# Hymba layer on one core: w_out blocks of the FFN's first output step through the ring, and four opening sums on VectorE

## The chip, the cores and the metric

The kernel runs on 1 core of one Trainium2 chip. The metric is the device time of one launch in microseconds (us); the time before is 2031.24 us, the median of 3 runs (2028.72 to 2032.04). The core has five engines with instruction queues of their own: TensorE (PE), VectorE (DVE), ScalarE (ACT), GpSimd (POOL) and SyncE (SP); in this kernel SP issues nearly all loads.

## The reference

One layer on 1024 tokens of width 1024, with 16 meta tokens put ahead of them and dropped at the end:

```python
h = h + 0.5 * swiglu(rms_norm(h, ffn1_norm), ffn1_w_in, ffn1_w_out)
u = rms_norm(h, mix_norm) @ w_in
o = concat([hgrn2(...), stick_breaking(...)])
h = h + o @ w_out
h = h + 0.5 * swiglu(rms_norm(h, ffn2_norm), ffn2_w_in, ffn2_w_out)

def swiglu(h, w_in, w_out):
    g, u = split(h @ w_in, 2)
    return (silu(g) * u) @ w_out
```

D_MODEL is 1024, D_FF is 2816 (22 tiles of 128, so 11 pairs). All in float32.

## The kernel before

**Products.** Every large product is exact to about float32: each operand is split into an upper half (a cast to fp32r on ACT) and a lower half (source minus upper half, on DVE), and PE runs three matmuls for each product, upper by upper, lower by upper, upper by lower. A block of 512 x 128 weights by 512 tokens is 12 matmuls of 128x512.

**Both FFNs** use a scheme with 7 products in place of 8 for 2 x 2 blocks (tokens in two halves, features in two halves). The left operands are block sums of the weights (A11, A12, S1 to S4, A22), the right ones are block sums of the activations (B11, B21, T1 to T4, B22). Each FFN has an input part, `fast_in` (columns of w_in, gate and up), and an output part, `fast_out` (w_out, steps over q = 0 to 10, a pair of 128 rows each).

**`fast_out`** runs its seven steps in the order A12, A11, S1, S2, S4, S3, A22. In each step and for each q, `left` gives the left block, `right` loads the activation from DRAM, `halved` makes upper and lower halves of both, and 12 matmuls follow (line 717, tile o). The program's order is static, engine by engine; each engine works through its own queue. Three kinds of place hold left blocks: `sk` and `ak` (11 places each, one for every q) and the ring, tag "raw", with `ring_bufs` places (7 in the first FFN, 6 in the second). A block in the ring is loaded by `raw` (line 629), one in sk by line 676. The place of sk in memory is used by another pool until shortly before: tiles `both`, sums of the second FFN's w_in, which the first FFN's middle makes ahead and stores to DRAM (`w2in`). In step A12 the first three q are one batch of 36 matmuls that goes over q within each product kind (`opening`). For the first FFN the flag `apart` is set, which keeps the halves of w apart in priority from those of the activations.

**`meta`** (inside the first FFN's part, line 1876 for its matmuls) carries the 16 meta tokens along as a narrow extra product. It uses each left block as long as that lies in memory: in A12 it holds the blocks back (`held`) and multiplies all 11 after q = 10, four matmuls each.

**The opening** (`open_tokens`) loads the tokens in rows, scales them by their norm (line 761, on DVE), turns them on PE (line 770, tile xps), and makes the right operands of the first FFN while PE already works on the first columns with B11 and B21. `items` lists what DVE and ACT do ahead of each product i of that stretch: 8 to 11 are `combine(0..3)` (lines 863 and 864), 12 to 15 are `second(0..3)`, which makes `t2[j]` = b22 - b11 (line 881) and the halves of T2 and T3. `prepare(0)` loads the four blocks of the first gate column and makes its four sums s1 to s4 (line 382). It is called in item 11 and runs on POOL; in other columns of the first FFN these sums are made on DVE.

**Names for the traces.** L479, L528, L535, L538 and L539 are the DVE additions behind the products qa, qb, qc of `fast_in`; L363 is the lower half of a left block there and L361 the upper; L643 and L644 are the upper and lower halves in `fast_out` (tiles w and t in the first FFN, parts in the second); L928 makes T4's differences after the opening; L311 is the lower half of a right operand.

Of the kernel before, what the change touches and what calls it, by code (L numbers as in the profile page):

```python
# [40 lines left out]
class Block:  # L41
# [309 lines left out]
    def fast_in(self, ops, n, w_in, actD, openers, ev0, open_ev, feed=None, meta=None, spare=None,  # L351
                between=lambda: None, after_opened=lambda: None, late=lambda: None, taken=lambda at, step=True: None):

        nc = self.nc
# [22 lines left out]
        def made(x, op, y, turns):  # L377
            if turns == 2:
                t = self.early_raw.tile([P, 4, P], F32, tag="raw", name="s", bufs=4)
            else:  # L380
                t = wp.tile([P, 4, P], F32, tag="s", name="s", bufs=3)
            taken(op(t, x, y), False)
            return t
# [14 lines left out]
        prepared = {}  # L398
        quarters = (0, 0), (1, 0), (1, 1), (0, 1)

        on = nc.vector if meta else nc.gpsimd

        def first_sums(blocks, turns, on):
            a11, a21, a22, _ = blocks
            s1 = made(a21, on.tensor_add, a22, turns)
            return s1, made(s1, on.tensor_sub, a11, turns)

        def prepare(col):
            blocks = [block(i, h, col) for i, h in quarters]
            a11, a21, _, a12 = blocks  # L410
            s1, s2 = first_sums(blocks, 2, nc.gpsimd)
            s3 = made(a11, nc.gpsimd.tensor_sub, a21, 2)
            prepared[col] = blocks, (s1, s2, s3, made(a12, nc.gpsimd.tensor_sub, s2, 2))

        def weights(col, opened, turns):
            if opened and feed:
# [194 lines left out]
    def fast_out(self, hT, cs, n, w_out, actD, ready, between=lambda a, q: None,  # L611
                 meta=lambda a, q, blocks: None):

        nc = self.nc
        op, ring, pout = self.op, self.ring, self.pout
        nq = D_FF // 256
        sk = op.tile([P, nq, 512], F32, name="sk")
        ak = op.tile([P, nq, 512], F32, name="ak")

        def block(i, j, q):  # L620
            f = 2 * q + j
            return w_out[f * P : (f + 1) * P, 512 * i : 512 * i + 512]

        def fresh():
            return ring.tile([P, 512], F32, tag="raw", name="raw", bufs=self.ring_bufs)

        def raw(i, j, q):
            t = fresh()
            nc.sync.dma_start(t, block(i, j, q))
            return t  # L630

        def right(key, n):
            t = ring.tile([P, n], F32, tag="act", name="act", bufs=self.act_bufs)
            nc.sync.dma_start(t, actD[key])
            return t

        turns = {"w": 0, "t": 0}

        def halved(src, name, m):
            i = turns[name]  # L640
            turns[name] = (i + 2) % 8
            hi, lo = (self.parts[name][:, j, :m] for j in (i, i + 1))
            nc.scalar.copy(hi, src)  # L643
            at = nc.vector.tensor_sub(lo, src, hi.bitcast(F32))  # L644
            if name == "w":
                los.append(at.ins)
            return hi, lo

        sub, los = nc.vector.tensor_sub, []

        def left(step, q):

            s, a = sk[:, q, :], ak[:, q, :]
            if step == "A11":
                nc.sync.dma_start(a, block(0, 0, q))
                return a, {(0, 0): a}
            if step == "S1":
                nc.vector.tensor_add(s, raw(1, 0, q), raw(1, 1, q))
                return s, {}
            if step == "S2":  # L660
                sub(s, s, a)
                return s, {}
            if step == "S4":
                t = raw(0, 1, q)
                sub(t, t, s)
                return t, {}
            if step == "S3":
                if self.apart:
                    nc.sync.dma_start(s, block(1, 0, q))
                    u = fresh()  # L670
                    sub(u, a, s)
                    return u, {(0, 0): a, (1, 0): s}
                sub(a, a, raw(1, 0, q))
                return a, {}
            if step == "A12":
                nc.sync.dma_start(s, block(0, 1, q))
                return s, {(0, 1): s}
            t = raw(1, 1, q)
            return t, {(1, 1): t}

        banks = {}
        delayed, opening = [], []

        def evict(bank, i, j, step, ms=range(4)):
            for m in ms:
                h = hT[:, 4 * i + m, cs[j] : cs[j] + n]
                nc.vector.scalar_tensor_tensor(
                    h, banks[bank][m], 0.5, h, ALU.mult, ALU.add
                )
            if 3 in ms:  # L690
                ready(step)

        steps = [
# [4 lines left out]
        ]  # L698
        for bank, a, b, start, (i, j) in steps:
            if start:  # L700
                banks[bank] = [
                    pout.tile([P, n], F32, tag=f"{bank}{m}", name="o") for m in range(4)
                ]
            for q in range(nq):
                with self.tc.issue_after(los[-4]) if self.apart and len(los) > 4 else ExitStack():
                    src, blocks = left(a, q)
                act = right((q, b), n)
                with self.tc.high_priority() if self.apart and a == "A12" and q < 3 else ExitStack():
                    wh, wl = halved(src, "w", 512)
                    xh, xl = halved(act, "t", n)  # L710
                order = [(m, e, q, wh, wl, xh, xl) for m in range(4) for e in range(3)]
                if a == "A12" and q < 3:
                    opening += order
                    order = sorted(opening, key=lambda o: (o[1], o[2])) if q == 2 else []
                for m, e, at, wh, wl, xh, xl in order:
                    y, z = ((wh, xh), (wl, xh), (wh, xl))[e]
                    nc.tensor.matmul(  # L717
                        banks[bank][m], y[:, m * P : (m + 1) * P], z,
                        start=start and at == 0 and e == 0,
                        stop=q == nq - 1 and e == 2, skip_group_check=True,  # L720
                    )
                meta(a, q, blocks)
                between(a, q)
                if q in (1, 3) and delayed:
                    evict(*delayed[0], range(q - 1, q + 1))
                    if q == 3:
                        delayed.pop()
            if a in ("S3", "A22"):
                evict(bank, i, j, a)
            else:  # L730
                delayed.append((bank, i, j, a))
# [43 lines left out]
    def open_tokens(self, ops, opened, prepare, rows_at, ev, operands):  # L775
# [9 lines left out]
        nc, x = self.nc, self.a["x"][0]  # L785
        stt, sub = nc.vector.scalar_tensor_tensor, nc.vector.tensor_sub
# [15 lines left out]
        def apart(name, pool):  # L802
# [4 lines left out]
        t2, b11, t3 = (apart(x, temps) for x in ("t2", "b11", "t3"))  # L807
        b22 = [ev.tile([P, 512], F32, tag=x, name="b22", bufs=1 + (x == "t"))
               for x in ("t", "t", "sg01", "sg10")]
# [51 lines left out]
        def combine(j):  # L861
            ps = kept["b12"][j]
            stt(b11[j], ps, g[j], b11[j], ALU.mult, ALU.subtract)
            stt(t3[j], ps, self.ng1[:, j : j + 1], b22[j], ALU.mult, ALU.add)

        def turn_meta():
            ps = self.pin.tile([P, KT, META], F32, tag="qd", name="mps", bufs=2)
# [8 lines left out]
        def second(j):  # L876
            if j == 0:
                rows_at.close()
                pools["masks"].close()
                operands("T1", "T3", "T2")  # L880
            sub(t2[j], b22[j], b11[j])
            self.halve(ops["T2"], t2[j], j)
            return self.halve(ops["T3"], t3[j], j)

# [23 lines left out]
            7: lambda: (keep_b22(), nc.vector.tensor_copy(self.masks, sd)),  # L908
        }
        items.update({12 + j: lambda j=j: second(j) for j in range(4)})  # L910
        items.update({8 + j: lambda j=j: combine(j) for j in range(3)})
        items[11] = lambda: (prepare(0), combine(3))
        after = {6: turn_b22, 7: turn_b12, 8: turn_meta}
        for i in range(2, len(order)):
            if i + 2 < len(order):
# [761 lines left out]
    def run(self):  # L1677
        nc, tc, a = self.nc, self.tc, self.a
# [20 lines left out]
        with ExitStack() as c0:  # L1699
            with ExitStack() as c1:  # L1700
# [8 lines left out]
                with tc.manual_schedule(engines={nc.tensor.engine}), ExitStack() as c2:  # L1709
# [98 lines left out]
                    opened, prepare = next(steps)  # L1808
# [13 lines left out]
                with tc.manual_schedule(engines={nc.tensor.engine}), ExitStack() as c2:  # L1822
# [59 lines left out]
                    last_q = D_FF // 256 - 1  # L1882
# [3 lines left out]
                    def meta(step, q, blocks):  # L1886
# [1 line left out]
                        if step not in banks_at:  # L1888
                            return
                        held.extend((i, j, q, t) for (i, j), t in blocks.items())  # L1890
                        if q < last_q and (step != "A22" or q % 3 < 2):
                            return
                        for i, j, at, t in sorted(held, key=lambda x: x[0]):
                            new = at == 0 and i in banks_at[step]
# [230 lines left out]
            with tc.manual_schedule(engines={nc.tensor.engine}), ExitStack() as cx:  # L2125
# [91 lines left out]
                made = feed()  # L2217
# [65 lines left out]
```

## Time and profile before

| | |
|---|---|
| runs | 2032.04, 2028.72, 2031.24 us |
| profiled execution | 2028.28 us, of which the span from the first to the last instruction is 2026.3 |
| granted TensorE clock, mean | 0.994 |
| w_in blocks of the first FFN's ring loads, us to landing (median) | 3.9 |
| w_out blocks: ring loads / sk loads (median) | 4.3 / 5.2 |

A line of the profile names the source line, engine, operation and tiles (out<-in) with their shapes, how often, the busy time and the mean of one, and after the bar the idle time ahead of it with what ended that. "SPq" is a DMA issue on SP's queue; "DMA x<-y" is the transfer itself. PEclk is the clock granted to TensorE, 1.00 being full speed. In a timeline a row holds the start, the duration, and the group of equal instructions that follow one another.

### The profile page before, as it was taken

The numbers are of one execution on the slowest core, as the hardware profiler recorded it, in microseconds if no ns is written. First come the engines' busy times: TensorE is split into PE (matmuls) and PEld (weight loads), VectorE is DVE, ScalarE is ACT, GpSimd is POOL, SyncE is SP. The second block draws the span as 40 slices with busy tenths as digits, with TensorE's granted clock in tenths as the row PEclk, the third lists the DMA queues.
The fourth block names the chain that finished last, engine by engine and source line by source line (L and its number), as shares of the span: only waits on it lengthen the run. The fifth ranks groups of instructions, "written<-read, shape, count | busy, mean of one in ns | idle before, by whom it ended". The sixth has DMA issues, their size and how long they took to land.

```text
span 2026.3 us, 30704 instructions
## 1 busy us (share of the span) xinstructions
PE 1960.7 (97%) x10940; PEld 1650.1 (81%) x10940; DVE 1364.6 (67%) x2136; ACT 860.6 (42%) x1731; POOL 462.6 (23%) x608
## 2 busy tenths in 40 slices
PE   7999999997999999999999999999999999989998
PEld 6788888885888888888888978877888888878887
DVE  7977777775578663247777667567566766757674
ACT  6523443333444444456666635433133332334443
POOL 4010100010000002233333331320544544520000
PEclk9999999998999999999999999999999999989999
DMA  6256787758955326344454166665533323278363
GB/s 205 86 160 170 250 272 244 236 182 306 331 189 187 126 70 188 129 160 116 123 144 138 50 255 175 165 220 178 185 98 104 111 94 104 98 264 291 112 200 135
DMA packets 315576, 347.16 MB, mean 171 GB/s; under 512 B 61520, under 2 KB 216656, under 8 KB 315424
## 3 DMA queue, kind: packets, MB, share of 16 engines
q1 hardware_dynamic: 297136, 292.18, 45.8%
q0 software_dynamic: 17248, 53.03, 7.6%
q8 instruction: 86, 1.41, 0.3%
q14 instruction: 66, 0.54, 0.1%
q10 hardware_dynamic: 1040, 0.00, 0.0%
HBM read 233.75 MB, written 111.38 MB: 170 GB/s over the span
## 4 chain that ended last, share of the span: by engine, by line
PE 90%; DVE 4%; DMA 3%; ACT 1%; issue 1%; SPq 0%; DVEq 0%; ACTq 0%
PE o L717 21%; PE qb L447 17%; PE qa L447 12%; PE qc L447 11%; PE proj L250 5%; PE proj L252 5%; PE proj L251 5%; PE flip L1409 2%; PE wo L250 1%; PE wo L251 1%; PE wo L252 1%; PE lvl L1202 1%; PE oacc L1479 1%; PE oacc L1481 1%; PE mq L981 1%; PE z L1545 1%
## 5 line engine op out<-in xcount | busy, mean ns | idle before, releaser
L447 PE MATMUL qb<-T,wh 128*128 128x512 f32 x1056 | 345.0, 391 | 2.6 <-DVE u L479 1.3
L447 PEld LDWEIGHTS qb<-T,wh 128*128 128x128 f32 x1056 | 198.2, 188 | 47.8 <-issue 2.5
L447 PE MATMUL qa<-B,wh 128*128 128x512 f32 x696 | 226.9, 391 | 0.3 <-ACT B L820 0.2
L717 PE MATMUL o<-t,w 128*128 128x512 f32 x924 | 213.0, 392 | 14.1 <-ACT w L643 14.1
L717 PE MATMUL o<-parts 128*128 128x512 f32 x924 | 212.8, 393 | 6.4 <-ACT parts L643 6.4
L250 PE MATMUL proj<-xh,wh 128*128 128x512 f32 (+2 forms) x640 | 216.7, 339 | 0.8 <-DVE st L1102 0.7
L717 PEld LDWEIGHTS o<-t,w 128*128 128x128 f32 x924 | 174.1, 189 | 51.0 <-ACT w L643 14.2
L252 PE MATMUL proj<-xl,wh 128*128 128x512 f32 (+2 forms) x640 | 209.9, 328 | 0.8 <-DVE xl L1864 0.8
L717 PEld LDWEIGHTS o<-parts 128*128 128x128 f32 x924 | 175.4, 190 | 43.4 <-ACT parts L643 6.8
L251 PE MATMUL proj<-xh,wl 128*128 128x512 f32 (+2 forms) x640 | 210.1, 328 | 0.0
L447 PE MATMUL qb<-T,wl 128*128 128x512 f32 x528 | 205.9, 390 | 1.2 <-DVE wl L363 1.2
L363 DVE TENSOR_TENSOR wl<-s,wh 128x512 fp32r<-128x512 f32 x160 | 165.8, 1036 | 50.2 <-ACT wh L361 49.2
L361 ACT CAST wh<-s 128x512 fp32r<-128x512 f32 x160 | 99.3, 622 | 194.1 <-PE qb L447 154.3
L447 PEld LDWEIGHTS qa<-B,wh 128*128 128x128 f32 x696 | 130.6, 188 | 27.9 <-DVE B L821 0.5
L361 ACT CAST wh<-raw 128x512 fp32r<-128x512 f32 x120 | 74.4, 621 | 147.3 <-PE qc L447 106.3
L447 PE MATMUL qa<-B,wl 128*128 128x512 f32 x348 | 135.6, 390 | 0.0
L252 PEld LDWEIGHTS proj<-xl,wh 128*128 128x128 f32 x640 | 120.7, 189 | 12.1 <-DVE xl L1864 1.2
L250 PEld LDWEIGHTS proj<-xh,wh 128*128 128x128 f32 x640 | 120.9, 189 | 11.3 <-DVE st L1102 1.2
L251 PEld LDWEIGHTS proj<-xh,wl 128*128 128x128 f32 x640 | 120.8, 189 | 9.0
L447 PE MATMUL qc<-B,wh 128*128 128x512 f32 x352 | 115.2, 391 | 2.2 <-DVE u L538 2.2
L447 PE MATMUL qc<-T,wh 128*128 128x512 f32 x352 | 117.2, 394 | 0.0
L447 PEld LDWEIGHTS qb<-T,wl 128*128 128x128 f32 x528 | 99.2, 188 | 21.6 <-DVE wl L363 1.6
(395 smaller groups left out, 3906.6 us busy)
## 6 DMA issues: line engine op xcount, KB each, us to landing
raw<-in_ffn_w_in_dram SPq DMA_DIRECT2D x176, 256.0 KB, 3.9
raw<-in_ffn_w_out_dram SPq DMA_DIRECT2D x99, 256.0 KB, 4.3
w2in<-both SPq DMA_DIRECT2D x28, 512.0 KB, 3.4
raw<-in_w_in_dram SPq DMA_DIRECT2D x25, 512.0 KB, 4.1
sk<-in_ffn_w_out_dram SPq DMA_DIRECT2D x33, 256.0 KB, 5.2
ks<-kD SPq DMA_DIRECT2D x32, 260.0 KB, 4.8
wout<-both SPq DMA_DIRECT2D x16, 512.0 KB, 3.6
wh<-w2in SPq DMA_DIRECT2D x27, 256.0 KB, 3.5
```

The costliest lines, as they stand in the source:

```text
L250: nc.tensor.matmul(ps, wh[:, s], xs, start=k == 0, stop=False)
L251: nc.tensor.matmul(ps, wl[:, s], xs, start=False, stop=False)
L252: nc.tensor.matmul(ps, wh[:, s], xl[:, k, c0 : c0 + n], start=False, stop=k == nk - 1)
L361: nc.scalar.copy(hi, src)
L363: nc.vector.tensor_sub(lo, src, hi.bitcast(F32))
L447: nc.tensor.matmul(ps, a[:, k, :], b[:, k, :], start=start and k == 0 and i == 0, stop=k == 3 and i == 2, skip_group_check=True,)
L717: nc.tensor.matmul(banks[bank][m], y[:, m * P : (m + 1) * P], z, start=start and at == 0 and e == 0, stop=q == nq - 1 and e == 2, skip_gro ...
L981: nc.tensor.matmul(ps[at : at + 32, at_g, :], self.xm[:, 4 * h + k, :], got[i, h][:, k, :], start=h == 0 and kk == 0, stop=h == 1 and kk = ...
L1202: nc.tensor.matmul(ps[:, :, c, :], kp[:, P * c : P * c + P], strided(QA, P * c + n, (512 - n, 2), (2 * n, nb), (1, n)), start=True, stop=True,
L1409: self.nc.tensor.transpose(ps[:m, j, :], src[:, s0 : s0 + m], self.ident)
L1479: nc.tensor.matmul(o[:, c], vj, w[0], start=j == 0, stop=False, skip_group_check=True)
L1481: nc.tensor.matmul(o[:64, c], vj[:, :64], w[1], start=False, stop=end, skip_group_check=True)
```

## The change

Three things are changed. (1) In step A12 of `fast_out`, the block of q goes to the ring by `raw(0, 1, q)` as long as q < `ring_bufs`, and to sk only from there on. (2) The meta tokens' matmuls of A12 are also issued after q = `ring_bufs` - 1, for the blocks held until then. (3) In the opening, `prepare(0)` is a generator that runs on `on`, which is DVE in the first FFN; `combine(0)`, `combine(1)` and `combine(2)` each take it one step further (loads with s1 and s2; s3; s4), and `combine(1..3)` make `t2[0..2]`, so `second` makes only `t2[3]`.

```diff
@@ prepare
-            s1, s2 = first_sums(blocks, 2, nc.gpsimd)
-            s3 = made(a11, nc.gpsimd.tensor_sub, a21, 2)
-            prepared[col] = blocks, (s1, s2, s3, made(a12, nc.gpsimd.tensor_sub, s2, 2))
+            s1, s2 = first_sums(blocks, 2, on)
+            yield
+            s3 = made(a11, on.tensor_sub, a21, 2)
+            yield
+            prepared[col] = blocks, (s1, s2, s3, made(a12, on.tensor_sub, s2, 2))
+            yield
@@ left
             if step == "A12":
-                nc.sync.dma_start(s, block(0, 1, q))
-                return s, {(0, 1): s}
+                if q >= self.ring_bufs:
+                    nc.sync.dma_start(s, block(0, 1, q))
+                    return s, {(0, 1): s}
+                t = raw(0, 1, q)
+                return t, {(0, 1): t}
@@ combine
             stt(t3[j], ps, self.ng1[:, j : j + 1], b22[j], ALU.mult, ALU.add)
+            if j:
+                sub(t2[j - 1], b22[j - 1], b11[j - 1])
+            if j < 3:
+                next(prepared)
@@ second
-            sub(t2[j], b22[j], b11[j])
+            if j == 3:
+                sub(t2[j], b22[j], b11[j])
@@ items
-        items.update({8 + j: lambda j=j: combine(j) for j in range(3)})
-        items[11] = lambda: (prepare(0), combine(3))
+        items.update({8 + j: lambda j=j: combine(j) for j in range(4)})
+        prepared = prepare(0)
@@ meta
-                        if q < last_q and (step != "A22" or q % 3 < 2):
+                        if q < last_q and (step, q) != ("A12", self.ring_bufs - 1) and (
+                            step != "A22" or q % 3 < 2
+                        ):
                             return
```

## The prediction

> **What bounds the kernel now.** I read the page first: the busy times, the chain that ended last, and the costliest groups with the idle time ahead of them.
>
> ```profile
> PE 1960.7 (97%) x10940; PEld 1650.1 (81%) x10940; DVE 1364.6 (67%) x2136; ACT 860.6 (42%) x1731; POOL 462.6 (23%) x608
> ...
> PE 90%; DVE 4%; DMA 3%; ACT 1%; issue 1%; SPq 0%; DVEq 0%; ACTq 0%
> ...
> L717 PE MATMUL o<-t,w 128*128 128x512 f32 x924 | 213.0, 392 | 14.1 <-ACT w L643 14.1
> L717 PE MATMUL o<-parts 128*128 128x512 f32 x924 | 212.8, 393 | 6.4 <-ACT parts L643 6.4
> ```
>
> TensorE (PE) is busy 97% of the 2026.3 us, so only some 65 us of idle time can be won at all. Two groups carry a lot of it: the w_out matmuls of the first FFN (tiles t, w) and of the second (parts). Each of the two amounts is one single wait, at the start of its step A12. Next I read, around the first, the waits (who waited for what: us in total, times, longest) and the chain.
>
> ```profile
> ACT w L643 <- DMA sk<-in_ffn_w_out_dram: 12.4, 1, 12.4
> ```
>
> ```profile
> 481.24 5.60 DMA w2in<-both
> ...
> 486.99 4.76 DMA sk<-in_ffn_w_out_dram
> ...
> 492.44 31.67 PE o L717 x132
> 524.11 2.54 PE m L1876 x88
> ```
>
> PE waits for a cast, the cast for the block's load into sk, and that load is issued only when a store of w2in has ended: the place of sk in memory is still being read by that store. The queue of SP and the last PE work ahead of the gap complete the picture (start, duration, what):
>
> ```profile
> 461.76 0.37 SPq L634 DMA_DIRECT2D act<-act10B  x1
> ...
> 468.68 4.01 SPq L629 DMA_DIRECT2D raw<-in_ffn_w_out_dram  x5
> ...
> 486.99 6.42 SPq L676 DMA_DIRECT2D sk<-in_ffn_w_out_dram  x11
> ```
>
> ```profile
> 477.82 0.53 PE L959 MATMUL mf<-pick,mt 128*128 128x32 f32 x4
> 492.44 31.67 PE L717 MATMUL o<-t,w 128*128 128x512 f32 x132 [14.09 <-ACT w L643]
> ```
>
> The ring already takes five blocks of w_out at 468.68, for the third step, S1, which is over 60 us away; the blocks that are needed at once come 18 us later.
>
> **The first transition, part by part.** After the change the blocks q = 0 to 6 of A12 go to the ring (seven buffers) by line 629, and SP's new order puts raw 0 into the slot of the first right-hand load, at 461.76, and the others between the next ones, all issued by about 472.5. Their landing, from the view of DMA issues over 455 to 500 us:
>
> ```profile
> raw<-in_ffn_w_out_dram SPq DMA_DIRECT2D x5, 256.0 KB, 5.3
> ```
>
> So all seven are there by 472.5 + 5.3 = 477.8, and the first three, which are enough for the opening 36 matmuls, by about 474, ahead of PE's end at 478.35. What is late next? The banks. Their last readers on VectorE (DVE) are these:
>
> ```profile
> 472.58 0.69 DVE L538 TENSOR_TENSOR u<-qc,u 128x512 f32<-128x512 f32 x1 [3.70 <-PE qc L447]
> ...
> 479.19 0.69 DVE L538 TENSOR_TENSOR u<-qc,u 128x512 f32<-128x512 f32 x1
> ```
>
> In the changed program's order DVE also takes three lower halves of w ahead of them, 3 x 0.6 = 1.8 us, which fit in its 3.70 us of idle time before 472.58 as far as the loads are early enough. The last bank is then free at 479.19 + 0.69 = 479.88 as before, at best 0.6 earlier, at worst 1.8 later. The first bank is free earlier, so PE starts between 478.7 and 480; I take a gap of 0.7 us, since only the last of four banks binds. The gap goes from 14.09 to 0.7: -13.4 (bounds -12.1 and -13.8).
>
> Next the granted clock after that gap. The columns are PE busy (matmuls), weight loads, DVE, ACT, POOL, the clock, the DMA share and GB/s:
>
> ```profile
> 492.00:494.00 2.00, 1.56 (x4) 1.28 (x5) 1.58 (x3) 1.90 (x4) 0.00 (x0) 0.50 1.05 387
> 494.00:496.00 2.00, 2.00 (x7) 1.57 (x6) 1.06 (x2) 0.34 (x1) 0.00 (x0) 0.60 1.04 393
> 496.00:498.00 2.00, 2.00 (x10) 1.64 (x10) 0.00 (x0) 0.10 (x1) 0.00 (x0) 1.00 1.05 399
> ```
>
> After 14 us of idleness PE runs at 0.50, and 132 matmuls take 31.67 us. One x512 matmul at full clock takes 0.227 us (12 in the 2.72 us of a block), so 132 would take 29.9: the cold start costs 1.7 us, and a gap of 0.7 us should not cause it. Some matmuls may also have waited for w in that time, so the bounds are 1.0 and 1.8. [...]
>
> Two more moves cost nothing by the rows, with their covers. The 28 of the 44 meta matmuls that move from behind q = 10 to behind q = 6 (the trace has two records for each, x88 in 2.54 us, so 1.6 us of it) are the same work on PE, at another place; they only need blocks that lie in the ring already. And the last four sk loads still wait for the w2in store until about 487 and land some 5 us later, 492; block 7 is wanted at 479 + 7 x 2.72 + 1.6 = 499.7. The cover is 7 us; gone, each us late is one us of PE.
>
> **The second transition.** fast_out is shared, and nothing in the condition asks for the first FFN. With the second FFN's ring of six buffers, q = 0 to 5 go to the ring there too. The rows:
>
> ```profile
> 1777.77 0.34 SPq L634 DMA_DIRECT2D act<-act0B  x1
> ...
> 1792.59 0.89 SPq L676 DMA_DIRECT2D sk<-in_ffn_w_out_dram  x1
> ```
>
> ```profile
> 1793.67 0.39 PE L447 MATMUL qc<-B,wh 128*128 128x512 f32 x1
> ```
>
> ```profile
> 1799.78 0.62 ACT L643 CAST parts<-sk 128x512 fp32r<-128x512 f32 x1 [10.78 <-DMA sk<-in_ffn_w_out_dram]
> ```
>
> ```profile
> 1794.09 0.69 DVE L538 TENSOR_TENSOR u<-qc,u 128x512 f32<-128x512 f32 x1 [1.30 <-PE qc L447]
> ```
>
> PE ends at 1794.06 and waits 6.4 us for a block whose load was issued at 1792.59. Raw 0 takes the slot at 1777.77, ahead of the first right-hand load; all six are issued by about 1788 and land before PE ends. The last bank is free at 1794.78, so the gap becomes 0.7: -5.7 (bounds -4.5 and -6.4). Its clock:
>
> ```profile
> 1800.00:1802.00 2.00, 1.55 (x4) 1.27 (x5) 1.54 (x3) 1.01 (x2) 1.22 (x3) 0.50 1.04 409
> 1802.00:1804.00 2.00, 2.00 (x6) 1.54 (x5) 1.97 (x3) 1.00 (x2) 1.04 (x1) 0.50 1.05 406
> 1804.00:1806.00 2.00, 2.00 (x6) 1.59 (x5) 1.47 (x2) 0.24 (x1) 0.86 (x2) 0.50 1.04 413
> 1806.00:1808.00 2.00, 2.00 (x9) 1.59 (x9) 0.00 (x0) 0.62 (x1) 0.00 (x0) 0.92 1.05 404
> ```
>
> In these 8 us PE runs 25 matmuls in 7.55 us of busy time, where 25 x 0.227 = 5.7 would do, and the next slice is still filling up; against full pace from 1800.45 on (118 matmuls in 29.8 us where 26.8 would do) it is 3.0 (bounds 1.9 and 3.0).
>
> **The opening.** Four sums of the first gate leave POOL. The rows of DVE, POOL and PE around them:
>
> ```profile
> 34.78 1.38 DVE L761 TENSOR_SCALAR row<-row,ss_x 128x1024 f32<-128x1024 f32 x2
> ...
> 36.70 3.43 DVE L761 TENSOR_SCALAR row<-row,ss_x 128x1024 f32<-128x1024 f32 x2
> ```
>
> ```profile
> 41.23 2.87 POOL L382 TENSOR_TENSOR s<-raw,s 128x512 f32<-128x512 f32 x1
> ```
>
> ```profile
> 38.50 0.66 PE L770 MATMUL xps<-ident,row 128*128 128x128 f32 x4 [1.00 <-DVE row L761]
> 40.18 0.66 PE L770 MATMUL xps<-ident,row 128*128 128x128 f32 x4 [1.02 <-DVE row L761]
> ```
>
> DVE scales a row of 1024 in 0.7 us until POOL starts its sums at 35.8, and in 1.7 us beside them; PE waits twice 1.0 us for these rows. Without POOL's sums, both waits should go: -2.0 (bounds 0, if something else slowed the rows, and -2.1).
>
> DVE gets four sums (0.6 us each back to back) and gets three of T2's differences earlier: 7 x 0.6 = 4.2 us more between 45 and 58, and 1.8 us fewer after 58.
>
> ```profile
> 40.00:50.00 10.00, 9.82 (x58) 8.23 (x59) 6.71 (x11) 4.15 (x7) 4.67 (x3) 1.00 0.27 79
> ...
> 60.00:70.00 10.00, 10.00 (x46) 8.29 (x45) 9.83 (x16) 7.84 (x16) 0.00 (x0) 1.00 0.22 62
> 70.00:80.00 10.00, 7.56 (x33) 5.62 (x32) 9.90 (x22) 5.35 (x11) 0.54 (x1) 1.00 0.06 26
> ```
>
> ```profile
> 58.71 0.69 DVE L881 TENSOR_TENSOR t<-b,b 128x512 f32<-128x512 f32 x1
> ```
>
> ```profile
> 74.73 0.50 PE L447 MATMUL qb<-T,wh 128*128 128x512 f32 x1 [1.28 <-DVE u L479]
> ...
> 79.12 0.50 PE L447 MATMUL qb<-T,wl 128*128 128x512 f32 x1 [1.16 <-DVE wl L363]
> ```
>
> DVE has 3.3 us idle in 40 to 50 and is full from 60 to 80, where PE waits 1.28 and 1.16 us for it. So the earlier work lies in idle time, and the full stretch gets 1.8 us shorter. But there DVE's order is changed as well: the lower half (line 363) that ended the second wait now stands behind two more subtractions of line 928 and a second u (line 479). I expect the two short waits to be replaced by one of about 2.5 us: net 0 (bounds -2.4, both gone, and +1.2, two more 0.6 us operations in front). The four block loads, too, move ahead of three on SP; those three are needed from 49 us on, and the queue has half its time free here, so 0.
>
> **The sum.** -2.0 - 13.4 - 1.7 - 5.7 - 3.0 = -25.8. The profiled execution took 2028.28 (its span of 2026.3 and 2.0 around it), 2.96 below the median of 2031.24. Its sum is 2002.5; set against the median I forecast 2005.4, say 2005. With all bounds at their best, -27.1 - 2.4 = -29.5 gives 2002 or, from the lowest run of 2028.72, 1999; at their worst, -19.5 + 1.2 = -18.3 gives 2013.
>
> **The rivals.** (1) Only the first transition closes, because the change is named for that FFN, or because DMA, at a share of 1.04 from 1800 on, still lands the second's blocks late. Against it: the SP slots from 1777.77 on lie well before that rush. Then 2031.24 - 17.1 = 2014. (2) The opening backfires: a sum waits on DVE for its block, all behind it waits too, and PE loses 2.5 us more and gains none of the 2.0: 2005.4 + 4.5 = 2010. [...] (3) The change does not do what it says: the loads are early, but PE restarts on the right-hand operand or a bank, and half of each gap (7.0 and 3.2) and the cold clock stay: 2031.24 - 10.2 - 2.0 = 2019. (4) Slower: S1 starves. The ring is now full of A12's blocks until q = 6, and S1's two blocks for each q, five of which were early before, are all loaded later. If only one pair were in flight, each of S1's 11 blocks would take 5.3 (landing) + 0.69 (sum) + 0.62 + 0.69 (halves) = 7.3 us against 2.72 on PE: +50 in the first FFN, 2005.4 + 50 = 2055. It decides when a pair takes over 2.72 + 25.8 / 11 = 5.1 us. Against it: six or seven buffers are three pairs in flight, 2.4 us a pair, and before, with 17 of the 22 blocks loaded at pace, the groups of line 717 show no wait but the two at their start.
>
> **How the numbers follow.** Chances: forecast 0.70, (1) 0.10, (2) 0.09, (3) 0.04, (4) 0.05, and 0.02 that gains and losses cancel. Faster by over 0.2% (4 us, about what a measurement tells from no change): 0.93; within: 0.02; slower: 0.05. The forecast's own range with the runs' scatter is 1999 to 2013; to take in (1) with the same scatter, 1999 to 2017.
>
> **What would show it.** Right: line 717's two groups with under 1.5 us of idle time each, clock 1.00 in the slices after both starts, no line 382 on POOL before 45 us and line 761 at 0.7 us throughout, a wait of 2 to 3 us near 75. Wrong: line 717 with a new releaser in steps S1 (DVE sk from raw, DMA raw), a wait of PE for line 363 in 45 to 58, or sk blocks 7 to 10 late.

## The result and the profile after

| | before | after |
|---|---|---|
| median of the runs beside each other, us | 2031.28 (2028.72 to 2032.04, 4 runs) | 2002.57 (2001.04 to 2003.36, 4 runs) |
| ratio, 95% interval | | 0.986 (0.9843 to 0.9877) |
| profiled execution / its span, us | 2028.28 / 2026.3 | 2002.59 / 2000.7 |
| mean granted clock | 0.994 | 0.999 |

The forecast was 2005 (1999 to 2017). Span against span the change takes 25.6 us off. The page of the changed kernel: busy times, chain, and the two groups of w_out matmuls (line 717 is line 723 now).

```profile
PE 1956.6 (98%) x10940; PEld 1646.5 (82%) x10940; DVE 1362.6 (68%) x2140; ACT 860.7 (43%) x1731; POOL 455.3 (23%) x604
...
PE 91%; DVE 4%; DMA 2%; ACT 1%; issue 1%; POOL 0%; SPq 0%; DVEq 0%; ACTq 0%
...
L723 PE MATMUL o<-t,w 128*128 128x512 f32 x924 | 212.1, 390 | 0.5 <-DVE u L541 0.5
...
L723 PE MATMUL o<-parts 128*128 128x512 f32 x924 | 209.9, 389 | 0.0
```

The idle time ahead of the first FFN's group fell from 14.1 to 0.5 us, that of the second from 6.4 to nothing. PE's busy time fell too, by 4.1 us for the same 10940 matmuls: the mean granted clock rose from 0.994 to 0.999. SP's queue and the chain of waits at the first transition (start, duration, what):

```profile
458.29 0.38 SPq L632 DMA_DIRECT2D raw<-in_ffn_w_out_dram  x1
460.93 0.32 SPq L637 DMA_DIRECT2D act<-act10B  x1
...
468.71 0.91 SPq L632 DMA_DIRECT2D raw<-in_ffn_w_out_dram  x2
...
485.23 0.88 SPq L680 DMA_DIRECT2D sk<-in_ffn_w_out_dram  x2
```

```profile
474.52 0.69 DVE u L541
...
475.34 8.86 PE o L723 x38
...
484.23 10.73 PE o L723 x46
494.96 1.67 PE m L1887 x56
496.63 11.12 PE o L723 x48
```

The seven ring loads are issued between 458.3 and 469.6, among the right-hand loads. No DMA stands in this chain any more: what PE waits for is the last reader of a bank on VectorE, 0.5 us. The sk loads are as late as they were (485 against 487), but nobody stands behind them. The meta tokens' matmuls are in two parts, 56 records at 494.96 and 32 later.

The clock behind both starts, at 475.34 and 1777.69 (columns as in the prediction's tables of stretches):

```profile
474.00:476.00 2.00, 1.52 (x10) 1.27 (x9) 2.00 (x4) 0.20 (x1) 0.54 (x1) 1.00 0.85 264
```

```profile
1778.00:1780.00 2.00, 2.00 (x11) 1.65 (x10) 1.67 (x3) 0.00 (x0) 0.22 (x2) 1.00 1.04 403
```

It stays at 1.00. DMA works at a share of about 1.0 as before, but PE no longer waits for it there.

In the opening, rows of DVE and of PE:

```profile
36.73 1.40 DVE L767 TENSOR_SCALAR row<-row,ss_x 128x1024 f32<-128x1024 f32 x2
```

```profile
36.50 2.34 PE L776 MATMUL xps<-ident,row 128*128 128x128 f32 x16
...
74.28 0.50 PE L450 MATMUL qb<-T,wl 128*128 128x512 f32 x1 [2.68 <-DVE wl L363]
```

Two rows are scaled in 1.40 us where they took 3.43, and PE's 16 matmuls that turn the four rows follow without a wait. Near 75 us one wait of 2.68 us has taken the place of 1.28 and 1.16.

### The profile page after: what moved, and what is told of

Same layout as the page of the kernel before. It is cut to its first block, busy times and chain, and to the rows that moved or that the text cites. A ratio compares the mean times of both kernels' runs of the same rounds, so it can differ in the third digit from the quotient of the medians.

```text
span 2000.7 us, 30716 instructions
## 1 busy us (share of the span) xinstructions
PE 1956.6 (98%) x10940; PEld 1646.5 (82%) x10940; DVE 1362.6 (68%) x2140; ACT 860.7 (43%) x1731; POOL 455.3 (23%) x604
## 4 chain that ended last, share of the span: by engine, by line
PE 91%; DVE 4%; DMA 2%; ACT 1%; issue 1%; POOL 0%; SPq 0%; DVEq 0%; ACTq 0%
PE o L723 21%; PE qb L450 17%; PE qc L450 12%; PE qa L450 12%; PE proj L250 5%; PE proj L252 5%; PE proj L251 5%; PE flip L1420 2%; PE wo L250 1%; PE wo L251 1%; PE wo L252 1%; PE mq L992 1%; PE lvl L1213 1%; PE oacc L1490 1%; PE oacc L1492 1%; PE z L1556 1%
## 5 line engine op out<-in xcount | busy, mean ns | idle before, releaser
L723 PE MATMUL o<-t,w 128*128 128x512 f32 x924 | 212.1, 390 | 0.5 <-DVE u L541 0.5
L723 PE MATMUL o<-parts 128*128 128x512 f32 x924 | 209.9, 389 | 0.0
L251 PE MATMUL proj<-xh,wl 128*128 128x512 f32 (+2 forms) x640 | 209.9, 328 | 0.0
L450 PE MATMUL qb<-T,wl 128*128 128x512 f32 x528 | 205.7, 390 | 2.7 <-DVE wl L363 2.7
```

The source lines that it names most:

```text
L251: nc.tensor.matmul(ps, wl[:, s], xs, start=False, stop=False)
L450: nc.tensor.matmul(ps, a[:, k, :], b[:, k, :], start=start and k == 0 and i == 0, stop=k == 3 and i == 2, skip_group_check=True,)
L723: nc.tensor.matmul(banks[bank][m], y[:, m * P : (m + 1) * P], z, start=start and at == 0 and e == 0, stop=q == nq - 1 and e == 2, skip_gro ...
```

## The experiments

The chips differ a little: the kernel before has a median of 2030.24 us (19 runs) beside the first four, 2033.18 (7 runs) beside the second four, and 2028.74 (7 runs) beside the last three. So ratios are compared, and spans where one execution's places are read. An edit is shown against the changed kernel's lines, and only in part where it says so.

| run | median us | ratio to before (95%) |
|---|---|---|
| first FFN's ring only | 2015.58 | 0.9929 (0.9915 to 0.9944) |
| second FFN's ring only | 2020.64 | 0.9955 (0.9940 to 0.9969) |
| opening only | 2028.52 | 0.9994 (0.9984 to 1.0005) |
| opening only, T2's differences late | 2028.41 | 0.9988 (0.9978 to 0.9997) |
| three blocks in the first ring | 2012.44 | 0.9905 (0.9887 to 0.9923) |
| meta matmuls not earlier | 2002.77 | 0.9859 (0.9842 to 0.9876) |
| T4's differences on GpSimd | 2002.69 | 0.9859 (0.9838 to 0.9880) |
| changed, T2's differences late | 2002.16 | 0.9851 (0.9833 to 0.9870) |
| one lower half first | 2004.43 | 0.9882 (0.9866 to 0.9899) |
| sums on GpSimd again | 2003.90 | 0.9883 (0.9868 to 0.9898) |
| changed kernel again | 2003.09 | 0.9884 (0.9868 to 0.9900) |

### One part at a time

The ring in the first FFN alone, with the opening as before (the one line of the ring is shown):

```diff
-                if q >= self.ring_bufs:
+                if not self.apart or q >= self.ring_bufs:
```

> The kernel before, with A12's early blocks in the ring (and the meta tokens' earlier matmuls) in the first FFN alone; opening and second FFN as before. Theory (the three gains are independent and each is what its own place shows): the wait of 14.1 us at the first w_out step becomes under 1 us and the cold clock behind it goes, 1.7 us; the 6.4 us at the second stay; 15.3 us less than before, about 2016. Rival (most of the gain sits in one place, since an earlier first FFN also moves the loads behind it): 20 us or more less, and the second wait shrinks without an edit.

```profile
L720 PE MATMUL o<-parts 128*128 128x512 f32 x924 | 212.5, 393 | 6.9 <-ACT parts L643 6.9
...
L720 PE MATMUL o<-t,w 128*128 128x512 f32 x924 | 212.0, 391 | 0.5 <-DVE u L538 0.5
```

The time is 0.71% less, 14.4 us of 2030.24, against 15.3 expected. The second wait stays, at 6.9 us: nothing shrinks there without its own edit, and the rival falls.

The ring in the second FFN alone, with the opening and the meta matmuls as before (again the one line):

```diff
-                if q >= self.ring_bufs:
+                if self.apart or q >= self.ring_bufs:
```

> The kernel before, with A12's early blocks in the ring in the second FFN alone. Theory: the wait of 6.4 us goes to 0 and some 2 to 3 us of half clock with it; 8 to 9.4 us less than before, about 2022.5, and the 14.1 us of the first stay. Rival (the half clock was no consequence of the wait, or the early start is given back later in that FFN): 6.4 us less or fewer, 2025 or above, with a clock of 0.5 or a new wait behind the start.

```profile
L720 PE MATMUL o<-t,w 128*128 128x512 f32 x924 | 213.4, 393 | 13.9 <-ACT w L643 13.9
...
L720 PE MATMUL o<-parts 128*128 128x512 f32 x924 | 209.9, 390 | 0.0
```

9.1 us less (0.45% of 2030.24). The wait of 6.4 us is gone, and the group's busy time fell from 212.8 to 209.9: 2.9 us more. That is the clock: in the profile before, PE works 5.86 us at 0.50 behind this wait, which is 2.9 us too long. The second FFN, which the change's name does not mention, is worth a third of the whole.

The opening alone (A12 and the meta matmuls as before), and the same with T2's differences left in `second` (that part of the edit is shown further down, under the changed kernel with T2's differences late):

```diff
-                if q >= self.ring_bufs:
+                if True:
...
-                        if q < last_q and (step, q) != ("A12", self.ring_bufs - 1) and (
-                            step != "A22" or q % 3 < 2
-                        ):
+                        if q < last_q and (step != "A22" or q % 3 < 2):
```

> The kernel before with the opening's edit alone (sums on VectorE in three steps, three of T2's differences early). Theory: the two waits of 1.0 us for scaled rows go, since GpSimd does no sums beside them; the two waits of 1.28 and 1.16 us near 75 us become one of 2.7; in all 2 us less, about 2029.3. Rival (what helps is the shorter stretch of VectorE after 58 us, from the early differences): the waits for rows stay, those near 75 us go.

> As the kernel with the opening's edit alone, but T2's differences stay where they were (behind the combinations, with the halves). Theory: the rows are scaled in 0.7 us all the same, as GpSimd's sums are gone (2.0 us gained before 41 us), but VectorE's full stretch from 58 us on is 1.8 us longer, so the wait near 75 us grows from 2.7 to about 4.5 us: about 2031, no gain. Rival (the differences' place does not matter, because VectorE makes the time up): the wait stays at 2.7 us and the time at 2029.

In both, PE's waits for rows are gone. Opening alone near 75 us, PE's row, and the chain behind the wait in this kernel (second fence) and in the changed one (third):

```profile
74.69 0.80 PE L450 MATMUL qb<-T,wl 128*128 128x512 f32 x1 [2.68 <-DVE wl L363]
```

```profile
74.69 7.04 PE qb L450 x23
```

```profile
74.28 5.53 PE qb L450 x23
```

The wait is the one of 2.7 us that was expected, and the changed kernel's profile has the same one. But here the clock falls to 0.50 behind it, from 74.6 to 78.0, and there it stays at 1.00: the same 23 matmuls take 7.04 us here and 5.53 there, so the clock cost 1.5 us in this execution. How the idle time lies in the two is in the last section.

With T2's differences late, PE's waits between 20 and 100 us, and the two groups:

```profile
PE qb L450 <- DVE u L482: 1.3, 1, 1.3
PE qb L450 <- DVE wl L363: 1.2, 1, 1.2
```

```profile
L723 PE MATMUL o<-t,w 128*128 128x512 f32 x924 | 213.6, 393 | 14.8 <-ACT w L646 14.8
L723 PE MATMUL o<-parts 128*128 128x512 f32 x924 | 212.3, 392 | 7.1 <-ACT parts L646 7.1
```

Neither theory nor rival is right: the wait near 75 us is neither 4.5 nor 2.7 but again 1.3 and 1.2, as before the change. VectorE makes up four more sums with its idle time; it is the early differences, not the sums, that turn two waits into one. The ratio 0.9988 is 2.4 us of 2030.24 (0.6 to 4.5), so the 2 us of the rows can be there in full; the 0.9994 of the opening alone is 1.2 us (-1.0 to 3.2). In this profile the two transitions wait 14.8 and 7.1 us, 0.7 more each than before, in that of the opening alone 13.7 and 6.0; one profile each does not say what moves them.

### What the ring must cover

Only three blocks in the first FFN's ring:

```diff
-                if q >= self.ring_bufs:
+                if q >= (3 if self.apart else self.ring_bufs):
```

> The changed kernel, but in the first FFN only the blocks q = 0 to 2 of A12 go to the ring and q = 3 to 10 to sk. Theory (it is the sk blocks, held up by the w2in stores until about 485 us, that set when PE can go on; the ring must cover the time until then): PE starts A12 at 475 as in the changed kernel, does 36 matmuls in 8.2 us, then waits some 5 to 8 us for block 3, and since that is longer than the clock lasts, PE runs at half clock again after it for 1.7 us; 2002.6 + 7 to 10, about 2011. Rival (three blocks are enough, the others only fill the ring): 2003.

```profile
476.99 8.41 PE L723 MATMUL o<-t,w 128*128 128x512 f32 x36 [0.48 <-DVE u L541]
492.69 13.26 PE L723 MATMUL o<-t,w 128*128 128x512 f32 x48 [7.29 <-ACT w L646]
```

```profile
488.00:490.00 2.00, 0.00 (x0) 0.00 (x0) 0.00 (x0) 0.00 (x0) 0.00 (x0) 0.99 1.12 379
490.00:492.00 2.00, 0.00 (x0) 0.00 (x0) 0.00 (x0) 0.00 (x0) 0.00 (x0) 0.50 0.92 320
```

As the theory had it: the start after the same wait of 0.5 us (in this execution 1.65 us later than in the changed kernel's), 36 matmuls, then 7.3 us for block 3 out of sk, and a cold clock (the group's busy time is 214.2 against 212.1). Together that is 9.4 us; the ratio is 0.45% above the changed kernel's, 9.1 us. PE idles from 485.4; the clock falls at 490. Three blocks gain the start and lose it 8 us later: the ring has to last until the sk blocks are there, at 492. At 2.72 us a block three more would have covered the 7.3 us, an estimate from these rows; four to six blocks were not tried.

### The ring's earlier release

The meta matmuls of A12 all behind q = 10 again (the edit of `meta` alone undone, as above):

> The changed kernel without the extra place for the meta tokens' matmuls: all 44 follow q = 10 again, so the seven ring buffers are held until then, some 11 us longer, and the third step's blocks can be loaded only later. Theory: the third step's first pair is wanted over 20 us after that, so nothing waits: 2002.6, same. Rival (this earlier release is what keeps the third step from starving, the slower case of the prediction): a wait of w_out matmuls for VectorE's sums or ring loads at the third step, 2 us or more slower.

Ring loads after A12 in this kernel (first row) and in the changed one (second row):

```profile
511.02 0.93 SPq L632 DMA_DIRECT2D raw<-in_ffn_w_out_dram  x2
```

```profile
505.39 0.96 SPq L632 DMA_DIRECT2D raw<-in_ffn_w_out_dram  x2
```

S1's loads start 5.6 us later, and the time is the same, 0.9859. The group of line 723 has 0.6 us of idle time in all. S1 does not starve, and this part of the change is worth nothing measurable.

### VectorE near 75 us

The changed kernel with T4's four differences on GpSimd:

```diff
-                    sub(b21[j], b21[j], t2[j])
+                    nc.gpsimd.tensor_sub(b21[j], b21[j], t2[j])
```

> The changed kernel with the four differences for T4 in the opening (b21 minus t2) on GpSimd, which is idle there, in place of VectorE. Theory (VectorE's amount of work between 58 and 90 us is what makes the one wait of 2.7 us): 2.4 us less on VectorE, the wait shrinks to 0.3 or less, 2 to 2.4 us faster, about 2000.3; GpSimd's operations (1.3 to 2 us each) end well before T4's halves are made. Rival (two-input work on GpSimd slows VectorE's operations beside it, as it did with the scaled rows): VectorE's operations beside it take over 0.8 us, and the wait stays or grows, 2002.6 to 2005.

```profile
54.46 1.61 POOL L939 TENSOR_TENSOR b<-b,t 128x512 f32<-128x512 f32 x1 [2.61 <-DVE t L872]
...
65.94 3.48 POOL L939 TENSOR_TENSOR b<-b,t 128x512 f32<-128x512 f32 x1 [5.54 <-DVE t L892]
```

```profile
54.84 1.78 DVE L363 TENSOR_TENSOR wl<-raw,wh 128x512 fp32r<-128x512 f32 x1
...
66.98 1.28 DVE L311 TENSOR_TENSOR T<-t,T 128x512 fp32r<-128x512 f32 x2
```

```profile
59.28 0.47 PE L450 MATMUL qa<-B,wh 128*128 128x512 f32 x1 [1.26 <-ACT wh L361]
```

Both happen. The wait of 2.7 shrinks to 0.3, so VectorE's amount of work did make it. But GpSimd takes each difference as soon as it can, from 50 us on; a lower half on VectorE beside it takes 1.78 us where it takes 0.68, and PE loses 1.26 us near 59, to an upper half on ScalarE that the changed kernel does not wait for (how the slowed operations make that one late was not followed). At 65.94 it is the other way: GpSimd's operation takes 3.48 us, where the others take 1.28 to 1.61, and VectorE's keep 0.6 each. What is left, 1.1 us, is below what the runs can tell: 0.9859 against 0.986.

The changed kernel with T2's differences late:

```diff
-            if j:
-                sub(t2[j - 1], b22[j - 1], b11[j - 1])
...
-            if j == 3:
-                sub(t2[j], b22[j], b11[j])
+            sub(t2[j], b22[j], b11[j])
```

> The changed kernel, but T2's differences stay where they were before (sums on VectorE, both rings). Theory (the early differences only turn two short waits near 75 us into one long one): waits of 1.3 and 1.2 us in place of 2.7, the time within 0.5 us of the changed kernel, 2002.4. Rival (now that nothing later swallows it, the early differences gain the 1.8 us that leave VectorE's full stretch): 2004.4.

```profile
PE qb L450 <- DVE u L482: 1.2, 1, 1.2
PE qb L450 <- DVE wl L363: 1.2, 1, 1.2
```

0.9851 against 0.986 of the changed kernel: no difference that the intervals tell. The early differences gain nothing here either.

The changed kernel with priority for the one lower half that PE waits for:

```diff
-            nc.vector.tensor_sub(lo, src, hi.bitcast(F32))
+            with self.tc.high_priority() if first_now[0] else ExitStack():
+                nc.vector.tensor_sub(lo, src, hi.bitcast(F32))
...
+                first_now[0] = bool(meta and opened and op == "T3")
                 left = ready.pop(0) if ready else next(w)
+                first_now[0] = False
```

> The changed kernel, with one lower half of a left block (line 363, the one that PE waits 2.7 us for near 74 us) given priority on VectorE, so that it comes ahead of the last halves of T1 and the differences for T4; no operation is added or moved to another engine. Theory (that wait is VectorE's order, not its amount of work: the operand was there early and stood behind four operations that nobody needed yet): the wait falls below 0.7 us and no other of over 1 us comes in its place before 100 us; 2 us faster than the changed kernel, 2000.5. Rival (VectorE is simply full until 90 us, so the 2.7 us come back at the next thing that it is late with): the same sum of PE's waits between 60 and 100 us, 2002.5.

```profile
76.86 0.54 PE L452 MATMUL qb<-T,wh 128*128 128x512 f32 x1 [2.09 <-ACT wh L361]
77.96 0.80 PE L452 MATMUL qb<-T,wl 128*128 128x512 f32 x1 [0.56 <-DVE wl L364]
```

```profile
77.17:84.00 6.83, 6.26 (x15) 4.79 (x15) 4.68 (x9) 3.99 (x8) 0.00 (x0) 0.50 0.00 0
```

The rival is right: the wait moves on by one product, to the next block's halves, with 2.09 + 0.56 = 2.65 us in place of 2.68. That block's sum (line 384 there) stands behind the postponed differences. In this execution the clock fell as well, for 6.8 us. Together with the smaller wait when T4's differences leave VectorE, this says that VectorE has more to do in this stretch than fits, and that the order only chooses what is late.

The changed kernel with the sums on GpSimd, in the same three places of the program:

```diff
-            s1, s2 = first_sums(blocks, 2, on)
+            s1, s2 = first_sums(blocks, 2, nc.gpsimd)
...
-            s3 = made(a11, on.tensor_sub, a21, 2)
+            s3 = made(a11, nc.gpsimd.tensor_sub, a21, 2)
...
-            prepared[col] = blocks, (s1, s2, s3, made(a12, on.tensor_sub, s2, 2))
+            prepared[col] = blocks, (s1, s2, s3, made(a12, nc.gpsimd.tensor_sub, s2, 2))
```

> The changed kernel with the first gate's four sums on GpSimd again, but in the changed places (behind the combinations, after the rows are scaled). Theory (what gains 2 us in the opening is that GpSimd does not work beside the scaling of the rows; which engine makes the sums is second): PE's waits for rows stay at 0; GpSimd's sums now run beside VectorE's two-input operations and slow some of them from 0.7 to 1.4 or 1.8 us, as the differences for T4 on GpSimd did, and that costs PE 0 to 2 us: 2002.5 to 2004.5. Rival (VectorE is the place that matters: with 2.4 us taken off it again, the wait of 2.7 us goes): 2000.

```profile
28.90 1.74 POOL L382 TENSOR_TENSOR s<-raw 128x512 f32<-128x512 f32 x1
30.61 2.25 POOL L382 TENSOR_TENSOR s<-raw,s 128x512 f32<-128x512 f32 x1
```

```profile
29.42 2.31 DVE L752 SCALAR_TENSOR_TENSOR junk<-row 128x1024 uint8<-128x1024 f32 x1
```

```profile
32.48 0.47 PE L450 MATMUL qa<-B,wh 128*128 128x512 f32 x1 [1.09 <-DVE sg L538]
```

The time lies within the theory's range (0.9883 beside 0.9884 for the changed kernel on the same chip), but the sums did not run where I had put them. GpSimd's queue is nearly empty, so it starts as soon as the blocks are there, at 26 us, now ahead of the scaling and beside the rows' sums of squares, one of which takes 2.31 us in place of 1.22. PE waits 1.09 us for what stands behind it, and still 2.37 near 75. The rows themselves are scaled at 0.7 us each, after GpSimd's last sum (it ends at 32.9), so what slows them in the kernel before is that GpSimd works beside them, not which engine makes the sums.

The changed kernel itself, beside the last two:

> The changed kernel itself, beside the two others on this chip. Every theory: 2002.6, one wait of 2.7 us near 74 us; whether the clock falls behind that wait may differ from the first profile (where it stayed 1.00), as it did in the kernel with the opening's edit alone (0.70).

```profile
74.02 0.50 PE L450 MATMUL qb<-T,wl 128*128 128x512 f32 x1 [2.69 <-DVE wl L363]
```

The same wait and, in this execution too, a clock of 1.00. No version tried is faster than the changed kernel beyond its interval.

## Why the prediction was right

**The sum.** Span against span, by terms: first wait 14.1 to 0.5, second 6.4 to 0, rows 2.0 to 0, the waits near 75 us 2.4 to 2.7, PE's busy time 4.1 less: -13.6 - 6.4 - 2.0 + 0.2 - 4.1 = -25.9, where the span shows -25.6 and -25.8 was forecast. That it comes so close is in part luck: 0.8 us too much for the first cold clock and 0.7 too little for the second wait cancel. The median moved by 28.7, since the profiled execution of before was faster than each of the four timed runs; beside the last three kernels the same change gives 1.16% of 2028.74, 23.5 us. The size is known to some 3 us, no better.

**First transition.** Forecast -13.4 for the wait, measured -13.6; the bank on VectorE is what is late next, as worked out. For the cold clock 1.7 was forecast, and the group's busy time fell by 0.9 only (213.0 to 212.1), just under my lower bound of 1.0. The clock itself cost what I had taken for it. In the profile before:

```profile
492.44:495.59 3.15, 3.15 (x8) 2.48 (x8) 2.62 (x4) 1.82 (x3) 0.00 (x0) 0.50 1.06 395
```

3.15 us at half the clock are 1.6 us lost, and the blocks behind them run at 2.72 us each. What I had at nothing is the rest: at a clock of 1.00 the changed kernel's first 132 matmuls take 8.86 + 10.73 + 11.12 = 30.7 us, not 29.9. About 0.3 us is a stop behind the 38th (484.23, a weight load that waits 0.4 us for VectorE's lower half of t), and about 0.3 the place where the meta tokens' matmuls now part the step once more, both estimates from the starts of the matmuls. So the move of the meta matmuls is not quite free, but it costs too little for the runs to tell. (The bound of -12.1 for the wait does not follow from its rows either: 1.8 us later than the 0.7 is a gap of 2.5, so -11.6.)

**Second transition.** Forecast -5.7 and -3.0, measured -6.4 and -2.9. The bank that I had expected to cost 0.7 us cost nothing. The 2.9 is what this wait cost in the one execution that I had sized it from: in the three other profiles that have the wait (first ring only, opening alone, opening with late differences) the group's busy time is 2.6, 1.8 and 2.4 above 209.9, for waits of 6.9, 6.0 and 7.1 us.

**Opening.** Rows: -2.0 forecast and measured, and the kernels without the ring show it too. That GpSimd's work beside VectorE was the reason is borne out by the two kernels that put some back: an operation of VectorE beside it took up to 1.9 (2.31 against 1.22 us) and 2.6 times as long (1.78 against 0.68), and the rows, scaled when GpSimd had ended, kept their 0.7 us. With T4's differences on GpSimd, VectorE's operation took 1.78 us at 54.84, where GpSimd had begun first (54.46), and GpSimd's took 3.48 us at 65.94, where VectorE had (65.78); what decides which of the two is slowed was not tried. The scaling of the rows is shown to slow down by its own rows alone (two in 1.38 us ahead of GpSimd's sums, two in 3.43 beside them). The exchange of two short waits for one of 2.5 us was right at 2.68. My reason for it was wrong in part: I had the sums and the differences together as work that shortens or fills VectorE's stretch; the run with late differences shows that the sums cost nothing and that the differences alone change the order.

**Rivals.** (1) falls with the second ring alone. (2), a wait of VectorE for a block, did not come. (3) falls with both groups. (4), a starving S1, has no sign even when its loads start 5.6 us later still; how late is too late was not tried.

**Not settled:** what the opening alone is worth in the time (0.9994, where its rows gain 2 us). The clock behind the one wait, 1.5 us where it falls, would account for the difference, and three of its ten runs have a mean clock of 0.992, which none has with late differences; but the intervals of the two kernels overlap. What moves the waits of the two transitions by up to 0.7 us between profiles is open as well.

## What to carry to other kernels

Where the matrix engine stands still at the seam of two phases, ask what holds the place that the first block is loaded to: a few blocks in buffers that are free early do for the whole seam, if they last until the held places come free, and shortage shows as the same wait a few blocks later. Count the cold clock with each such wait (half the clock cost 1.6 us behind the one of 14.1 us here, 2.9 behind the one of 6.4), and do not join two short waits into one long one for nothing: the long one, 2.68 us, cost the clock 1.5 us in the opening alone, where the two of 1.3 and 1.2 did not. An edit of the order in a stretch where VectorE is full only moved the wait here, 2.65 us in place of 2.68. Work that went to an idle GpSimd ran when its inputs had landed (from 26.3 us the sums, from 50.3 the differences), not where the program has it, and while it and VectorE ran side by side, one slowed the other (1.78 us in place of 0.68 on VectorE, 3.48 in place of 1.28 to 1.61 on GpSimd).

## What the runs showed of the hardware

**Where the granted clock changed.** The wait of 2.68 us (or 2.69) near 75 us stands in five profiles. The clock stayed at 1.00 in three (changed kernel, changed again, three blocks) and fell for 3.41 us in two (opening alone, meta matmuls not earlier): PE's two qb groups are busy 344.3 to 344.7 and 205.6 to 205.7 us in the three, 345.5 to 345.8 and 206.4 to 206.6 in the two. In the profile of the kernel before, the clock is 0.50 from 481.94 to 495.59 and from 1796.07 to 1806.31; those are four and three steps of 3.413 us, and from the first fall to the second there are 385. In opening alone it is 0.50 from 74.60 to 78.02, one step, in one lower half first from 77.17 to 84.00, two. So in these three profiles the changes lie on a grid of 3.413 us. Laid over PE's work (its busy time is the first number behind the comma, in us), here is one step each of six profiles, in this order: opening alone (with the cold step behind it), meta matmuls not earlier, changed, changed again, before, and first ring only:

```profile
71.19:74.60 3.41, 0.82 (x4) 0.36 (x2) 3.41 (x7) 1.78 (x3) 0.00 (x0) 1.00 0.00 0
74.60:78.02 3.42, 3.33 (x8) 2.69 (x9) 3.05 (x6) 1.66 (x3) 0.00 (x0) 0.50 0.00 0
```

```profile
71.88:75.29 3.41, 1.36 (x6) 1.14 (x7) 3.41 (x7) 1.58 (x4) 0.00 (x0) 1.00 0.00 0
```

```profile
72.85:76.26 3.41, 1.98 (x9) 1.64 (x10) 3.41 (x7) 1.96 (x4) 0.00 (x0) 1.00 0.00 0
```

```profile
72.32:75.73 3.41, 1.71 (x7) 1.42 (x8) 3.41 (x7) 1.69 (x4) 0.00 (x0) 1.00 0.00 0
```

```profile
1792.65:1796.07 3.42, 1.41 (x7) 0.83 (x5) 1.53 (x3) 0.00 (x0) 1.01 (x2) 1.00 0.85 256
```

```profile
1779.90:1783.31 3.41, 1.47 (x7) 0.89 (x5) 1.59 (x3) 0.00 (x0) 0.94 (x2) 1.00 0.76 243
```

At the end of the step the clock fell in opening alone (2.59 us idle), meta not earlier (2.05) and before (2.01), and stayed in changed (1.43), changed again (1.70) and first ring only (1.94). In before and changed, step by step from PE's first matmul on, no step with more than 1.63 us of idle time kept the clock, and none with less than 2.01 lost it (to about 0.1 us, as the ends of matmuls are modelled). So the wait of 2.7 us went with a fall in opening alone and in meta not earlier, where 2.59 and 2.05 us idle lie in one step, and with none in changed and changed again, where 1.43 and 1.70 do; the grid lies elsewhere in each execution. The clock came back at the end of steps with 0.26 and 0.00 us of idle time in before, not at the end of one with 0.96, and in opening alone at the end of one with 0.09. Two waits of 1.2 to 1.3 us, with matmuls between them, put at most 1.28 us into one step in before, and in none of the five profiles that have them did the clock fall there (their qb groups are busy 344.7 to 345.1 and 205.6 to 205.9 us); 2.09 us, one matmul and 0.56 us (one lower half first) lost it for two steps.

**How long PE had stood still when the clock fell.** With three blocks in the ring PE stood still from 485.4 and the clock fell 4.6 us later, at 490.0; before the change it fell 3.6 us (first transition) and 2.0 us (second) after PE's last matmul, and with the first ring only 5.4 us (second).
